# An encoder block on one Trainium2 core: where the last gate/up block turns its second pair, and where the last row of x joins its bank

## The chip, the cores and the metric

The kernel runs on one core of one Trainium2 chip. Its engines work side by side, each through its own list of instructions in order: TensorE (PE, matrix products into the eight PSUM banks), VectorE (DVE), ScalarE (ACT), GpSimd (POOL, which here mostly issues DMAs) and SyncE (SP, which issues the loads of weights). ACT and DVE also read PSUM. The metric is the time of one execution on the device in microseconds (us), a median over runs.

## The reference

One layer on x of 512 tokens by 2048, in float32:

```python
h = rmsnorm(x, g_mix)
qa, ka, va, qb, kb, vb = split(h @ w_in)
out_a = rmsnorm(mixer_a(qa, ka, va), g_out_a)   # grouped-query attention, axial rotary
out_b = rmsnorm(mixer_b(qb, kb, vb), g_out_b)   # three dilated windows, merged
x = x + concat(out_a, out_b) @ w_out
gate, up = split(rmsnorm(x, g_ffn) @ w_gate_up) # 2048 -> 2 x 5632
x = x + (silu(gate) * up) @ w_down              # 5632 -> 2048
return rmsnorm(x, g_final)
```

## The kernel before

**Products.** Each float32 factor is split into a high and a low part, and `mm3` makes a product from three matmuls of 128x128 by 128x512 (L228, L229, L230). The weights' high part is made by ACT (L837), the low part by DVE (L840), into tiles named `wide`. The large products go by a scheme of seven forms instead of eight blocks, named m1 to m7. A form is a sum of blocks of the activations times a sum of blocks of the weights (DVE makes the latter at L973). The forms share PSUM banks: m1, m6, m5 and m3 build on one another in the two banks of "z", m7 and m4 in those of "y", m2 in those of "x". So when m6 is complete its banks are read out, and m5 then accumulates onto the same banks.

**Units.** The program is a list of units; in the gate/up and down products a unit is one pair of rows of one form, six matmuls. The instructions of all engines are written out unit by unit. `box.after(form, late, f)` calls `f` `late` units behind the last unit of that form; the count runs on into the next block. This sets the order on every engine; there is no further scheduler.

**Gate/up and down.** Eleven gate/up blocks (`gate_up_block`) make four groups of 128 columns of silu(gate) * up each, as tiles `glo` and `uhi`. These must be turned (tokens from partitions to columns) to be the activations of the down product. The first ten blocks turn by DMA, the last one by PE: `turn_on_pe(k)` transposes one group with four matmuls (L1270) into a spare PSUM bank, and ACT copies it to a half of the tile `pair` (L1271). There is one such tile, `hpart[0]`. After two groups, `pair_sums` makes the sums that the forms need (four operations of DVE at L379), and `store` writes all seven forms of the pair to DRAM by a DMA from POOL (L1275). `next_forms` loads forms from there (`fr`, L1324) and splits them on ACT and DVE (L1327, L1330) into the `arena`.

The down product goes in blocks of 6, 8 and 8 pairs, twice each (two halves of the output's columns). The first block, of 6 pairs, has 42 units in this order: m1 and m7 mixed (12), m6 (6), two of m2, m5 (6), m2 and m4 mixed (6), m4 and m3 mixed (10). It begins right behind the last gate/up block, so "18 units behind m3" is the last unit of m6, and 34 units behind it the first unit of m3.

When a form of a down block is complete, ACT reads its two banks out (L1357), scaled, into an eviction tile from the ring `evs`, and POOL issues DMAs that add the tile to the output in DRAM (`x1d`, L1358). The ring begins with four tiles (`s6` and `ev`, two each). The four tiles of `s1` and `s7`, which hold `glo` and `uhi` until they are turned, join it later by the hook at L1473.

**The end.** The last down block does not write to DRAM; `put_row` (L1417) adds the banks to rows of x on the chip. Its m3 does the first row of tokens unit by unit and the second in `finish`, all at once, on a bank to which `seed_last` (L1443 to L1445, DVE) has added that row of x, divided by the row's scale. The row, `x1[3, 1]`, is the last of the rows that POOL loads from `x1d` (L1312). The order of this block is m1, m7, m6, two of m2, m5, m4, the rest of m2, m3, eight units a form.

Of the kernel before, what the change touches and what calls it, by code (L numbers as in the profile page):

```python
# [76 lines left out]
def encoder_block(ctx, tc, x, w_in, g_q_a, g_k_a, w_out, w_gate_up, w_down, g_final, x_t, gains, c_ident, c_mask,  # L77
# [36 lines left out]
    def small(n=4):  # L114
        used[0] += n
        assert used[0] <= 512
        return fixed[:, used[0] - n:used[0]]
# [118 lines left out]
    twins, evs, frs = [], [], []  # L236
# [919 lines left out]
    def pair_sums(w):  # L1156
        def part(n):
            return w[:, n * 256:(n + 1) * 256]
        a_r, a_l, s3, s2, b_l, b_r, s1, s4 = (part(n) for n in range(8))
        form_sums(a_l, a_r, b_l, b_r, s1, s2, s3, s4)  # L1160
# [41 lines left out]
    held = {}  # L1202

    def hold(name, shape, dtype=F32):
        if name not in held:
            held[name] = sp.tile([P] + list(shape), dtype, tag=name, bufs=1, name=nm(name))
        return held[name]

    forms_dram = dp.tile([P, 7, NFF // 2, 256], F32, tag="forms", name="forms")
    def gate_up_block(f0):  # L1210
        box = ColBlock(w_gate_up, 0, (f0 * P, DFF + f0 * P), KD // 2, REREAD, "craw40" if f0 == 40 else "craw", hf if f0 == 0 else None, two=True)
# [54 lines left out]
        def turn_on_pe(k):  # L1266
            ps, half = bank(), k % 2
            for n, t in enumerate((2, 3, 0, 1) if half == 0 else range(NT)):
                src = st[("glo", "uhi")[t // 2]][t % 2][:, k * P:(k + 1) * P]
                nc.tensor.transpose(ps[:, n * P:(n + 1) * P], src, ident)  # L1270
            nc.scalar.activation(hpart[0][:, half * 1024:half * 1024 + 512], ps, AF.Copy)  # L1271
            release(ps)

        def store(n):
            nc.gpsimd.dma_start(forms_dram[:, :, n], hpart[0][:, 256:].rearrange("p (f c) -> p f c", c=256))  # L1275
# [9 lines left out]
        box.after("m3", 1, low)  # L1285
        box.after("m3", 3, high)
        if f0 + 4 == NFF:
            for k, late in enumerate((6, 8, 18, 20)):
                box.after("m3", late, lambda k=k: turn_on_pe(k))
                if k % 2:  # L1290
                    box.after("m3", late + 2, lambda: pair_sums(hpart[0]))
                    box.after("m3", late + 5, lambda k=k: store((f0 + k) // 2))
            return box
# [10 lines left out]
    for f in range(0, NFF, 4):  # L1304
        box = gate_up_block(f)
# [3 lines left out]
    def load_x1(c, rows):  # L1309
        for t in rows:  # L1310
            x1.setdefault((c, t), slot("x1"))
            nc.gpsimd.dma_start(x1[c, t], x1_dram[c, t])  # L1312
# [31 lines left out]
    def down_block(first, pairs, cb, last):  # L1344
        box = ColBlock(w_down, 2 * first * P, (cb * 1024, cb * 1024 + 512), pairs, KEPT, f"draw{pairs}",
                       close=finish if last else None, two=True)

        def add(form, i, j):
            def go():
                for t in range(2):  # L1350
                    row = 2 * i + t
                    if not evs:
                        evs.extend(held["s6"][:, t] for t in range(2))
                        evs.extend(hold("ev", [2, 512])[:, t] for t in range(2))
                    evs.append(evs.pop(0))
                    e = evs[-1]
                    nc.scalar.activation(e, box.bank_of(form)[t], AF.Copy, scale=r2["r"][:, row:row + 1])  # L1357
                    nc.gpsimd.dma_start(x1_dram[2 * cb + j, row], e, accum_op=OP.add)  # L1358
                if form in LAST_OF_BANK:
                    box.done(form)  # L1360
            box.after(form, 0, go)

        def put(form, i, j):
            box.after(form, 0, lambda: [put_row(2 + j, 2 * i + t, box.bank_of(form)[t]) for t in range(2)])

        add("m1", 0, 0)
        add("m7", 1, 1)
        add("m6", 1, 0)
        if last:
            done_rows = [(c, t) for c in range(2) for t in (2, 3, 0, 1)]  # L1370
            for n in range(2):
                box.after("m7", 2 + 3 * n, lambda n=n: [load_gfin(n), load_x1(n, (2, 3)), load_x1(n, (0, 1))])
            box.after("m7", 7, lambda: [load_gfin(c) for c in (3, 2)])
            for n, (c, t) in enumerate(done_rows):
                box.after("m6", n - 2, lambda c=c, t=t: squares(c, t))
                box.after("m6", n, lambda c=c, t=t: gained(c, t))
            box.after("m6", 2, lambda: [load_x1(c, rows) for c, rows in ((3, (2, 3)), (2, (2, 3)), (2, (0, 1)), (3, (0, 1)))])
            put("m5", 1, 1)
            put("m4", 1, 0)
            box.after("m2", 0, last_weights)  # L1380
            put("m2", 0, 0)
            for t in range(2):
                box.after("m4", -4 + t, lambda t=t: gained(3, 2 + t))
                box.after("m2", 1 + t, lambda t=t: gained(2, t))
            box.after("m4", 1, lambda: [row_scale(t) for t in (2, 3)])
            box.after("m2", 3, lambda: seed_last(box.bank_of("m3")[1]))
            for n, (t, c) in enumerate(((2, 0), (2, 1), (3, 0), (3, 1))):
                box.after("m4", 2 + n, lambda t=t, c=c: [write(t, c, False, nc.sync), write(t, c + 2, True, nc.sync)])
        else:
            add("m2", 0, 0)  # L1390
            add("m5", 1, 1)
            add("m4", 1, 0)
            add("m3", 0, 1)
        return box
# [9 lines left out]
    def load_gfin(c):  # L1404
        gfin[c] = slot("gfin")
        nc.gpsimd.dma_start(gfin[c], row_bcast(g_final[c * 512:(c + 1) * 512], 512))
# [6 lines left out]
    def squares(c, t):  # L1413
        nc.scalar.activation(slot("jf"), x1[c, t], AF.Square, accum_out=sums_of(t)[:, c:c + 1])

    def put_row(c, t, ps):
        nc.vector.scalar_tensor_tensor(x1[c, t], ps, r2["r"][:, t:t + 1], x1[c, t], op0=OP.mult, op1=OP.add)  # L1417
        squares(c, t)

    def gained(c, t):  # L1420
        nc.vector.tensor_tensor(x1[c, t], x1[c, t], gfin[c], op=OP.mult)
        fin["y", c, t] = True

    def row_scale(t):
        tot = small(1)
        nc.vector.tensor_reduce(tot, fin[t], axis=AX.X, op=OP.add)
        fin["r", t] = rsqrt_mean(tot, 1, D)

    def write(t, c, vector, queue):
        r, y = fin["r", t], x1[c, t]  # L1430
        if ("y", c, t) not in fin:
            nc.vector.scalar_tensor_tensor(y, y, r, gfin[c], op0=OP.mult, op1=OP.mult)
        else:
            y = y if fin["y", c, t] is True else fin["y", c, t]
            if vector:
                nc.vector.tensor_scalar(y, y, r, None, op0=OP.mult)
            else:
                nc.scalar.activation(y, y, AF.Copy, scale=r)
        queue.dma_start(out[0, t * P:(t + 1) * P, c * 512:(c + 1) * 512], y)

    def seed_last(ps):
        r, q = r2["r"][:, 1:2], small(2)
        nc.vector.reciprocal(q[:, :1], r)  # L1443
        nc.vector.tensor_scalar(q[:, 1:], r, D ** -0.5, None, op0=OP.mult)
        nc.vector.scalar_tensor_tensor(ps, x1[3, 1], q[:, :1], ps, op0=OP.mult, op1=OP.add)  # L1445
        fin["mean"] = q[:, 1:]
# [23 lines left out]
        nc.vector.scalar_tensor_tensor(x1[3, 1], ps[1], m[:, 2:3], gfin[3], op0=OP.mult, op1=OP.mult)  # L1470
        nc.scalar.dma_start(out[0, P:2 * P, 3 * 512:], x1[3, 1])

    box.after("m3", 24, lambda: evs.extend(held[name][:, t] for name in ("s1", "s7") for t in range(2)))  # L1473
    first = 0
    for n in DOWN_PAIRS:
        next_forms(box, first, n)
        for cb in range(2):
            box = down_block(first, n, cb, (first + n, cb) == (NFF // 2, 1))
        first += n
# [149 lines left out]
```

## Time and profile before

| | before |
|---|---|
| median of 3 runs | 1963.26 us (1961.18 to 1963.49) |
| profiled execution | 1964.77 us, span 1963.0 us |
| instructions | 24580 |
| mean granted clock of TensorE | 0.996 |
| moved by DMA | 409.30 MB, 209 GB/s |

The span runs from the first to the last instruction of one profiled execution; the execution's time also has what lies around it. All times within the trace count from the span's start. An engine's busy time is the sum of its instructions; in a row of a timeline the bracket gives the time that the engine stood before the instruction, and what ended it. The granted clock is the share of TensorE's full clock that was let through.

### The profile page before, as it was taken

To read this page: it belongs to the slowest core of one execution; us is meant where nothing else is said; L and a number is where in the kernel's file an instruction comes from. 1 tells how busy PE (TensorE), PEld (TensorE's weight loads), DVE (VectorE), ACT (ScalarE), POOL (GpSimd) and SP (SyncE) were. 2 spreads that over 40 slices of the span, in tenths; PEclk is the share of its full clock that TensorE was granted. 3 is DMA by queue.
4 is the path that set the end of the run, shared out by engine and by line. 5 is a ranking of instruction groups with operands and counts; after the bars stand their busy time and mean duration, and the time that the engine had idled before them with its cause. 6 is when DMAs were issued, how large, how long until landed. Compare 5 with 4: busy or idle time off the path is not lost.

```text
span 1963.0 us, 24580 instructions
## 1 busy us (share of the span) xinstructions
PE 1941.8 (99%) x8743; PEld 1604.0 (82%) x8743; DVE 1536.9 (78%) x2012; ACT 1122.6 (57%) x1643; POOL 139.6 (7%) x184
## 2 busy tenths in 40 slices
PE   9999999999999999999999999999999899999998
PEld 7888888888888888888888888888888688888886
DVE  7987768787775697778778778778788778787886
ACT  7755554565455565555555555555555566555555
POOL 0000011000000000000000000000000121111121
PEclk9999999999999999999999999999999899999999
DMA  9677693144343566858758758767679688868865
GB/s 344 226 268 231 210 283 108 58 150 150 102 150 97 172 208 188 295 146 278 260 153 283 243 171 279 225 198 279 202 222 334 152 224 270 224 162 247 236 143 169
DMA packets 252028, 409.30 MB, mean 209 GB/s; under 512 B 58688, under 2 KB 85824, under 8 KB 251776
## 3 DMA queue, kind: packets, MB, share of 16 engines
q1 hardware_dynamic: 221072, 321.12, 50.1%
q0 software_dynamic: 22480, 60.57, 12.4%
q10 hardware_dynamic: 8352, 26.05, 4.1%
q8 instruction: 68, 1.11, 0.2%
q14 instruction: 56, 0.46, 0.1%
HBM read 334.52 MB, written 62.65 MB: 202 GB/s over the span
## 4 chain that ended last, share of the span: by engine, by line
PE 91%; issue 4%; DVE 3%; DMA 1%; ACT 1%; POOL 0%; DVEq 0%; POOLq 0%; SPq 0%; ACTq 0%
PE b L228 30%; PE b L229 30%; PE b L230 30%; PE b L613 1%; DMA forms<-pair 0%; PE b L1171 0%; PE b L563 0%; DVE x L1125 0%; PE b L790 0%; DVE w L306 0%; DVE ra L460 0%; DVE tw L896 0%; POOL x1d L1358 0%; DVE qA L463 0%; DMA stage<-in_w_in_dram 0%
## 5 line engine op out<-in xcount | busy, mean ns | idle before, releaser
L837 ACT ACTIVATE wide<-raw 128x1024 fp32r<-128x1024 f32 x462 | 487.0, 1059 | 456.5 <-PE b L230 271.1
L228 PE MATMUL b<-wide,arena 128*128 128x512 f32 x1848 | 721.7, 391 | 9.0 <-ACT s L1357 8.3
L840 DVE TENSOR_TENSOR wide<-raw,wide 128x1024 fp32r<-128x1024 f32 x462 | 562.1, 1221 | 213.9 <-ACT wide L837 207.5
L229 PE MATMUL b<-wide,arena 128*128 128x512 f32 x1848 | 720.8, 390 | 0.0
L230 PE MATMUL b<-wide,arena 128*128 128x512 f32 x1848 | 720.6, 390 | 0.0
L228 PEld LDWEIGHTS b<-wide,arena 128*128 128x128 f32 x1848 | 347.8, 188 | 81.4 <-ACT s L1357 8.6
L230 PEld LDWEIGHTS b<-wide,arena 128*128 128x128 f32 x1848 | 347.8, 188 | 72.3
L229 PEld LDWEIGHTS b<-wide,arena 128*128 128x128 f32 x1848 | 347.9, 188 | 71.6
L973 DVE TENSOR_TENSOR raw<-raw,raw 128x1024 f32<-128x1024 f32 x264 | 321.0, 1218 | 6.6 <-DMA raw<-in_w_gate_up_dram 6.6
L229 PE MATMUL b<-tw,arena 128*128 128x512 f32 x396 | 154.4, 390 | 0.6 <-DVE tw L896 0.6
L230 PE MATMUL b<-tw,arena 128*128 128x512 f32 x396 | 154.2, 389 | 0.0
L228 PE MATMUL b<-tw,arena 128*128 128x512 f32 x396 | 154.2, 389 | 0.0
L893 ACT ACTIVATE tw<-stage 128x512 fp32r<-128x512 f32 x140 | 85.4, 628 | 69.3 <-DVE stage L973 44.4
L896 DVE TENSOR_TENSOR tw<-stage,tw 128x512 fp32r<-128x512 f32 x140 | 93.5, 685 | 23.2 <-ACT tw L893 23.1
L228 PE MATMUL b<-w,arena 128*128 128x512 f32 x240 | 95.9, 400 | 0.0
L219 ACT ACTIVATE pTh<-b 128x512 fp32r<-128x512 f32 x64 | 38.2, 597 | 99.9 <-PE b L613 98.2
L230 PE MATMUL b<-w,arena 128*128 128x512 f32 x240 | 94.0, 392 | 0.0
L229 PE MATMUL b<-w,arena 128*128 128x512 f32 x240 | 93.6, 390 | 0.0
L229 PEld LDWEIGHTS b<-tw,arena 128*128 128x128 f32 x396 | 74.4, 188 | 16.8 <-DVE tw L896 1.4
L228 PEld LDWEIGHTS b<-tw,arena 128*128 128x128 f32 x396 | 74.4, 188 | 15.5
L230 PEld LDWEIGHTS b<-tw,arena 128*128 128x128 f32 x396 | 74.4, 188 | 15.2
L379 DVE TENSOR_TENSOR pair<-pair 128x256 f32<-128x256 f32 x120 | 46.4, 421 | 46.6 <-ACT pair L1174 23.2
(234 smaller groups left out, 2097.9 us busy)
## 6 DMA issues: line engine op xcount, KB each, us to landing
raw<-in_w_gate_up_dram SPq DMA_DIRECT2D x308, 512.0 KB, 6.2
raw<-in_w_down_dram SPq DMA_DIRECT2D x88, 512.0 KB, 7.7
stage<-in_w_in_dram SPq DMA_DIRECT2D x111, 256.0 KB, 5.4
forms<-pair POOLq DMA_DIRECT2D x22, 896.0 KB, 6.5
fr<-forms ACTq DMA_DIRECT2D x35, 512.0 KB, 5.0
raw<-in_w_out_dram SPq DMA_DIRECT2D x32, 512.0 KB, 4.2
x1d<-s POOLq DMA_DIRECT2D x56, 256.0 KB, 6.8
stage<-in_w_in_dram SPq DMA_DIRECT2D x90, 128.0 KB, 3.5
```

The lines of the kernel that those rows point to most:

```text
L219: nc.scalar.activation(hi, src, AF.Copy)
L228: nc.tensor.matmul(dst, ah, bh, start=start, stop=False, skip_group_check=chained)
L229: nc.tensor.matmul(dst, ah, bl, start=False, stop=False, skip_group_check=chained)
L230: nc.tensor.matmul(dst, al, bh, start=False, stop=stop, skip_group_check=chained)
L379: nc.vector.tensor_tensor(out, x, y, op=op)
L613: nc.tensor.transpose(ps[:, t * P:(t + 1) * P], self.p[t][:, kb * P:(kb + 1) * P], ident)
L837: nc.scalar.activation(self.hi, self.src, AF.Copy)
L840: nc.vector.tensor_tensor(self.lo, self.src, f32(self.hi), op=OP.subtract)
L893: nc.scalar.activation(self.pair[:, 0], self.src, AF.Copy)
L896: nc.vector.tensor_tensor(self.pair[:, 1], self.src, f32(self.pair[:, 0]), op=OP.subtract)
L973: nc.vector.tensor_tensor(t[dst], t[src[0]], t[src[1]], op=OP.add if form == "m6" else OP.subtract)
```

## The change

Three hooks are given other places. In the last gate/up block (`f0 + 4 == NFF`) the third and fourth group are turned 34 and 36 units behind its m3 instead of 18 and 20; the sums follow two units and the store five units behind the fourth group, so they move along. The tiles of `s1` and `s7` join the eviction ring 40 units behind it instead of 24. In the last down block, `seed_last` is called five units behind m5 instead of three behind m2.

```diff
         if f0 + 4 == NFF:
-            for k, late in enumerate((6, 8, 18, 20)):
+            for k, late in enumerate((6, 8, 34, 36)):
                 box.after("m3", late, lambda k=k: turn_on_pe(k))
                 if k % 2:
                     box.after("m3", late + 2, lambda: pair_sums(hpart[0]))
                     box.after("m3", late + 5, lambda k=k: store((f0 + k) // 2))
...
-            box.after("m2", 3, lambda: seed_last(box.bank_of("m3")[1]))
+            box.after("m5", 5, lambda: seed_last(box.bank_of("m3")[1]))
...
-    box.after("m3", 24, lambda: evs.extend(held[name][:, t] for name in ("s1", "s7") for t in range(2)))
+    box.after("m3", 40, lambda: evs.extend(held[name][:, t] for name in ("s1", "s7") for t in range(2)))
```

The order on ACT around the end of m6 in the first down block; `b_78` and `b_71` are the banks of the turned groups, `b_72` and `b_76` those of m6, `s_546` an eviction tile:

```order
 L1327 ACTIVATE arena_85<-fr_10982 128x4x256
 L837 ACTIVATE wide_5846<-raw_5908 128x1024
-L1271 ACTIVATE pair_5381<-b_78 128x512
 L1357 ACTIVATE s_546_6203<-b_72,fixed 128x512
 L1357 ACTIVATE s_546_6203<-b_76,fixed 128x512
 L837 ACTIVATE wide_5840<-raw_5739 128x1024
 L1324 DMA fr_10982<-forms 128x1024
-L1271 ACTIVATE pair_5381<-b_71 128x512
 L1327 ACTIVATE arena_85<-fr_10983 128x2x256
```

The copy of the third group stood ahead of the evictions of m6 and stands there no more; that of the fourth has gone from behind them.

ACT sixteen units later, behind the evictions of m2, and ahead of those of m4:

```order
 L837 ACTIVATE wide_5846<-raw_5906 128x1024
+L1271 ACTIVATE pair_5381<-b_75 128x512
 L837 ACTIVATE wide_5840<-raw_5940 128x1024
+L1271 ACTIVATE pair_5381<-b_71 128x512
 L837 ACTIVATE wide_5842<-raw_5908 128x1024
```

Both copies now stand here, each between two splits of weights, out of banks `b_75` and `b_71`.

POOL's DMAs in the same part; `s_546` and `ev` are eviction tiles, and the rows with `x1d` add them to the output in DRAM, for m2, m4 and m3 in turn:

```order
 L1358 DMA x1d_122<-s_546_6203 128x512
 L1358 DMA x1d_123<-s_546_6203 128x512
+L1358 DMA x1d_124<-ev_11330 128x512
+L1358 DMA x1d_125<-ev_11330 128x512
+L1275 DMA forms<-pair_5381 896x1x256
+L1358 DMA x1d_126<-s_546_6203 128x512
+L1358 DMA x1d_127<-s_546_6203 128x512
```

The second pair's store, which stood behind m6's DMAs, now stands between those of m4 and m3, and these two take their tiles from the ring of four (before, they had `s1` and `s7`).

DVE in the last down block; `b_77` is the bank that the seed goes to, `x_638` the last row of x:

```order
 L840 TENSOR_TENSOR wide_5847<-raw_13693,wide_5846 128x1024
 L1421 TENSOR_TENSOR x_632_13748<-x_632_13748,gfin_13703 128x512
+L1443 RECIPROCAL fixed<-fixed 128x1
+L1444 TENSOR_SCALAR fixed<-fixed 128x1
+L1445 SCALAR_TENSOR_TENSOR b_77<-x_638_13760,fixed,b_77 128x512
 L840 TENSOR_TENSOR wide_5841<-raw_13723,wide_5840 128x1024
```

The three operations of the seed stood ahead of the last `put_row`, behind all splits of weights; they now have six splits behind them.

## The prediction

> **What bounds the kernel now.** The page comes first, then the waits of TensorE (PE):
>
> ```profile
> PE 1941.8 (99%) x8743; PEld 1604.0 (82%) x8743; DVE 1536.9 (78%) x2012; ACT 1122.6 (57%) x1643; POOL 139.6 (7%) x184
> PE 91%; issue 4%; DVE 3%; DMA 1%; ACT 1%; POOL 0%; DVEq 0%; POOLq 0%; SPq 0%; ACTq 0%
> PE b L228 <- ACT s L1357: 8.3, 1, 8.3
> PE b L228 <- DVE b L1445: 0.6, 1, 0.6
> ```
>
> PE is busy for 99% of the span and makes 91% of the chain that ended last, so a microsecond in which PE does not wait is a microsecond of the span, and hardly anything else is. PE waits long only once, 8.3 us, for the eviction at L1357; the other wait that the change touches is 0.6 us for the seed at L1445. The timelines of the engines show how the long one comes about (start, length, engine, line, idle time before it and what ended it):
>
> ```profile
> 1536.07 1.54 DVE L379 TENSOR_TENSOR pair<-pair 128x256 f32<-128x256 f32 x4
> 1542.43 1.74 POOL L1358 DMA_DIRECT2D x1d<-ev  x2 [4.31 <-ACT ev L1357]
> 1550.31 0.94 POOL L1275 DMA_DIRECT2D forms<-pair  x1 [6.14 <-DVE raw L973]
> 1546.40 1.06 ACT L837 ACTIVATE wide<-raw 128x1024 fp32r<-128x1024 f32 x1 [0.26 <-DVE raw L973]
> 1557.88 0.60 ACT L1271 ACTIVATE pair<-b 128x512 f32<-128x512 f32 x1 [10.42 <-DMA forms<-pair]
> 1558.37 1.26 ACT L1357 ACTIVATE s<-b,fixed 128x512 f32<-128x512 f32 x2
> 1550.19 0.60 PE L1270 MATMUL b<-fixed,s 128*128 128x128 f32 x4
> 1559.11 0.79 PE L228 MATMUL b<-wide,arena 128*128 128x512 f32 x1 [8.32 <-ACT s L1357]
> ```
>
> The first pair's sums (L379) were done at 1537.6, but its store was issued only at 1550.31, 6.1 us after POOL's accumulating DMAs, and landed at about 1557.8. ACT's copy of the second pair (L1271) writes the same single tile `pair`, so it stood from 1547.5 to 1557.88 for that landing. Queued right behind it were the evictions of m6's banks (L1357), which PE needs before m5 may accumulate there. PE stood until 1559.11 and then ran slowly. Busy time and instructions by engine (PE, PEld, DVE, ACT, POOL), then granted clock, DMA share and GB/s:
>
> ```profile
> 1555.00:1559.10 4.10, 0.00 (x0) 0.00 (x0) 0.00 (x0) 1.22 (x3) 0.00 (x0) 0.51 0.45 164
> 1559.10:1565.30 6.20, 6.19 (x15) 4.84 (x16) 4.66 (x8) 3.59 (x6) 1.77 (x2) 0.50 0.87 165
> 1565.30:1570.00 4.70, 4.70 (x22) 3.91 (x21) 4.65 (x5) 3.10 (x4) 0.94 (x1) 1.00 0.76 227
> ```
>
> After the stand PE had half its clock for 6.2 us more: 15 matmuls there, 22 in the shorter stretch behind it.
>
> **The change part by part.** *The second pair's turn, 16 units later.* The waiting copy no longer stands ahead of m6's evictions on ACT (first piece of the order above). What they now wait for is PE's end of m6, at about 1547.1, so both are done by about 1548.7, while PE has two units of m2 (12 matmuls, 2.7 us) before m5. The gain is read from the starts of PE's matmuls:
>
> ```profile
> 1546.98 0.60 PE L1270 MATMUL b<-fixed,s 128*128 128x128 f32 x4
> 1547.33 0.48 PE L228 MATMUL b<-wide,arena 128*128 128x512 f32 x1
> 1549.96 0.39 PE L230 MATMUL b<-wide,arena 128*128 128x512 f32 x1
> 1565.51 0.40 PE L228 MATMUL b<-wide,arena 128*128 128x512 f32 x1
> ```
>
> Behind four transposes the next matmul starts after 0.35 us (1546.98 to 1547.33). Behind those at 1550.19 it took 8.92 us, so the stand costs 8.92 - 0.35 = 8.57 us. From 1559.11 to 1565.51 are 15 starts, 6.40 us. At full clock, 11 starts took 2.63 us (1547.33 to 1549.96), and four more at 0.23 us make 3.55 for 15. The slow clock therefore costs 6.40 - 3.55 = 2.85 us. With PE never idle here, nothing in the trace would lower the clock: the share is 1.00 in every stretch of this stage in which PE does not stand.
>
> The Trainium skill's page "TensorE: Matmul & The Clock Gate" (Part 1: The HAM clock gate) says that the clock halves after an idle window of about 3.4 us and is whole again after about 3.4 us of work. The halving agrees (0.51 and 0.50 after the stand); the length does not, 6.2 us here. By the page's length the clock term would be an estimated 1.7 us instead of 2.85, and the time 1.15 us later than I forecast.
>
> The transposes, the two copies and the sums are moved, not added. The copies now come behind m2's evictions, the store behind m4's DMAs and ahead of m3's (second and third piece). PE's transposes take two banks that nothing has used since the first pair's turn, so PE does not wait for them. ACT's loads of `fr`, which stood behind the waiting copy, leave earlier, and none stands behind it at the new place; SP's order is the same. The copy still waits for the first store. Sixteen units of six matmuls at 0.23 us are 22 us, so it comes at about 1569, and the landing at 1557.8 has 11 us to spare. For what lies beside it:
>
> ```profile
> 1545.00:1550.00 5.00, 5.00 (x26) 4.12 (x25) 5.00 (x6) 2.20 (x3) 0.00 (x0) 1.00 0.98 193
> 1570.00:1575.00 5.00, 5.00 (x23) 4.15 (x23) 2.09 (x2) 3.02 (x5) 1.73 (x2) 1.00 0.99 261
> 1580.00:1585.00 5.00, 5.00 (x23) 4.13 (x22) 3.46 (x3) 3.88 (x5) 1.73 (x2) 1.00 0.95 288
> 1585.00:1590.00 5.00, 5.00 (x24) 4.13 (x22) 2.63 (x4) 2.71 (x5) 1.39 (x2) 1.00 1.07 318
> 1600.00:1605.00 5.00, 5.00 (x24) 4.15 (x23) 4.63 (x4) 2.41 (x4) 0.11 (x1) 1.00 0.05 11
> ACT wide L837 <- DMA raw<-in_w_down_dram: 0.3, 1, 0.3
> 1565.89 0.94 POOL L1275 DMA_DIRECT2D forms<-pair  x1 [4.67 <-issue]
> 1571.72 0.87 POOL L1358 DMA_DIRECT2D x1d<-ev  x1 [4.88 <-ACT ev L1357]
> ```
>
> The four sums (1.54 us) leave a stretch where VectorE (DVE) had no free time (5.00 of 5) and enter one with 3.9 us free in ten (1580 to 1590): price zero. If that cover were gone, at most 1.54; nothing to win either, since PE did not wait where they were. The copies (two of 0.6) find ACT 3.4 us free there. In the gap DVE stood too, waiting for ACT; what it loses is the 2.85 us of slow matmuls in which it could get ahead. Between 1570 and 1575 it was idle 2.9 us for want of work, so I take zero and keep 2.85 as the upper end.
>
> The store moves past three pairs of accumulating DMAs on POOL. A store and the DMA behind it were 5.8 us apart (1565.89 to 1571.72), so m3's pair may leave some 10 us later than before: the store first waits for m4's pair to land, as the first one did. Their tiles are wanted again a whole block later. Its own 0.9 MB meets full DMA engines (1.07), but ACT waited for weights only 0.3 us in this stage, and at 1600 to 1605 they stand empty. Zero again, with 1 us as the upper end, as no PE wait came from weights.
>
> *The eviction ring.* Until unit 40 it has four tiles, so m3's eviction reuses the tile of m2's:
>
> ```profile
> 1579.76 1.25 ACT L1357 ACTIVATE s<-b,fixed 128x512 f32<-128x512 f32 x2
> 1580.72 1.73 POOL L1358 DMA_DIRECT2D x1d<-s  x2 [7.27 <-ACT s L1357]
> 1591.56 1.37 ACT L1357 ACTIVATE s<-b,fixed 128x512 f32<-128x512 f32 x2 [0.81 <-PE b L230]
> DMA to landing us min/median/max: 4.0/6.5/10.0
> ```
>
> The last row is for the accumulating DMAs between 1530 and 1610. By the median, m2's pair lands at about 1588; by the longest at 1591.4, just ahead of 1591.56. I take zero. The upper end is a wait of a few us on ACT, of which PE sees only what exceeds ACT's lead; in the old wait PE stood 8.32 of ACT's 10.42, so the lead was 2.1.
>
> *The seed.* It moves on DVE from m3's third unit to m4's fifth (last piece). The tail in starts of PE's matmuls, and what lies beside the new place:
>
> ```profile
> 1947.90 0.39 PE L229 MATMUL b<-wide,arena 128*128 128x512 f32 x1
> 1948.13 0.39 PE L230 MATMUL b<-wide,arena 128*128 128x512 f32 x1
> 1949.16 0.50 PE L228 MATMUL b<-wide,arena 128*128 128x512 f32 x1 [0.64 <-DVE b L1445]
> 1949.97 0.39 PE L228 MATMUL b<-wide,arena 128*128 128x512 f32 x1
> 1925.00 1.70 POOL L1312 DMA_DIRECT2D x<-x1d  x3 [0.42 <-issue]
> x<-x1d POOLq DMA_DIRECT2D x16, 256.0 KB, 4.6
> 1934.28 1.43 DVE L1417 SCALAR_TENSOR_TENSOR x<-b,fixed,x 128x512 f32<-128x512 f32 x2 [2.39 <-PE b L230]
> ```
>
> From 1948.13 to 1949.97 are four starts in 1.84 us; at 0.23 each they take 0.92, so 0.92 us goes, and the final chain hangs on PE's last matmul. The last row of x comes with the last of the loads at 1926.2, so with 4.6 us at about 1930.8, when DVE reaches the seed (about 1930.6). A late row holds the weights' split behind it, covered by the 2.39 us that DVE stood before 1934.28. Lower end zero, upper 0.92; I take 0.92.
>
> **The sum.** 8.57 + 2.85 + 0.92 = 12.3 us. The profiled execution took 1964.77 (span 1963.0, 1.8 around it): 1952.4 after. It lies 1.5 over the median of the runs, 1963.26, to which I refer the forecast: 1951.0.
>
> **The rivals.** (a) *The cover is gone*: with PE running on, DVE and ACT come late between 1550 and 1600. For it speaks DVE's 5.00 of 5; against it, that PE waited for no split there, and that DVE had idle time 20 us later. Price 2.85 to 4.4 (plus the sums' 1.54), so 1954 to 1955.5; with a second loss of clock 1957. A store that delays weights ends in the same place. The page "DMA: Bandwidth & Descriptors" (Queues, rings and completion order) says that each DMA engine takes turns between queues packet by packet, so by it the store does slow the loads beside it; no row here gives that price.
>
> (b) *The change does not remove the wait*: something else holds m6's evictions as long. The copy was the only instruction ahead of them that waited for a DMA, and nothing replaces it. Only the seed's gain would stay: 1962.3.
>
> (c) *Slower*: the ring of four tiles. If m2's pair lands late, ACT stands at m3's eviction with the weights' copies behind it. To lose more than was won, PE would have to stand over 9.5 us (2.85 of clock on top), ACT over 11.6, so the landing would be at 1603, some 21 us after the issue; the longest took 10.0. If so, 1964 to 1967.
>
> **Chances.** The forecast 0.77, its own range 1949.5 to 1953.1: 1.2 us to each side for the runs' spread (1961.18 to 1963.49), 0.92 up if the seed brings nothing, 0.25 down if the clock costs half of its whole 6.2 us. (a) 0.14, (b) 0.05, (c) 0.04. The range for 8 in 10 reaches into (a): 1949.0 to 1955.5 (half a us below the forecast's own). This kernel's measurement can tell about 0.2%, 3.9 us, from no change. The forecast and (a) lie beyond that, 0.91 faster; (b) is the same, with a little of (c), 0.06; the rest of (c) 0.03 slower.
>
> **What the profile after should show.** No PE wait for L1357; granted clock 1.00 from 1530 to 1600; m5's first matmul right behind m2's second unit; ACT's L1271 of the second pair ended by PE's transposes instead of the store; the second store issued once m4's DMAs have landed; no PE wait for L1445. The prediction is wrong if PE waits for L840, L837 or an eviction between 1550 and 1610, or if DVE stands for `x<-x1d` at the seed for over 2.4 us.

## The result, and the profile after

The changed kernel takes 1952.09 us (median of 4 runs, 1951.01 to 1953.56) against 1962.3 of the kernel before in the same comparison (1961.18 to 1963.49): ratio 0.9948, 95% interval 0.9931 to 0.9966. It is 10.2 us faster, 0.34 to 0.69%. The forecast was 1951.0 with a range of 1949.0 to 1955.5. The profiled execution took 1951.23 us, its span 1949.4.

The page after (engines, then the chain):

```profile
PE 1937.3 (99%) x8743; PEld 1599.7 (82%) x8743; DVE 1536.5 (79%) x2012; ACT 1123.3 (58%) x1643; POOL 140.1 (7%) x184
PE 96%; DVE 3%; issue 1%; ACT 0%; DMA 0%; DVEq 0%; POOLq 0%; POOL 0%; SPq 0%; ACTq 0%
```

The longest waits of PE over the whole run (waited for: us in total, times, longest):

```profile
PE b L186 <- DVE warm L181: 1.3, 1, 1.3
PE b L229 <- DVE tw L896: 0.6, 2, 0.3
```

PE has gone from 91 to 96% of the chain, and the waits for L1357 (8.3 us) and L1445 (0.6) are gone. From 1500 to 1960 no wait of PE is left at all. The timelines of ACT, POOL and DVE at the places that were changed:

```profile
1546.10 1.25 ACT L1357 ACTIVATE s<-b,fixed 128x512 f32<-128x512 f32 x2
1568.26 0.59 ACT L1271 ACTIVATE pair<-b 128x512 f32<-128x512 f32 x1
1571.43 0.60 ACT L1271 ACTIVATE pair<-b 128x512 f32<-128x512 f32 x1 [0.70 <-PE b L1270]
1578.95 1.37 ACT L1357 ACTIVATE s<-b,fixed 128x512 f32<-128x512 f32 x2 [0.81 <-PE b L230]
1548.72 0.94 POOL L1275 DMA_DIRECT2D forms<-pair  x1 [5.82 <-DVE raw L973]
1557.58 1.77 POOL L1358 DMA_DIRECT2D x1d<-s  x2 [7.92 <-ACT ev L1357]
1584.90 0.94 POOL L1275 DMA_DIRECT2D forms<-pair  x1 [6.97 <-DVE wide L840]
1589.91 1.76 POOL L1358 DMA_DIRECT2D x1d<-s  x2 [4.06 <-ACT wide L837]
1917.73 0.76 DVE L1445 SCALAR_TENSOR_TENSOR b<-x,fixed,b 128x512 f32<-128x512 f32 x1
```

m6's evictions start at 1546.10, not 1558.37, and no longer stand behind a copy. The copies (L1271) wait for PE's transposes at most, no longer for the store. The second store leaves 6.97 us behind POOL's issue for m4, m3's DMAs at 1589.91, 9.6 us after ACT was done with that tile (1580.3), and nobody waits for them: m3's eviction itself waited only for PE. The seed runs at 1917.73 without a wait. By stretches (columns as before: length; PE, PEld, DVE, ACT, POOL; granted clock, DMA share, GB/s):

```profile
1545.00:1550.00 5.00, 5.00 (x24) 4.14 (x23) 5.00 (x6) 3.74 (x6) 0.94 (x1) 1.00 0.88 210
1555.00:1560.00 5.00, 5.00 (x24) 4.14 (x23) 4.69 (x4) 4.17 (x6) 2.42 (x3) 1.00 0.84 271
```

PE is busy throughout at a granted clock of 1.00, with DVE close to full.

**Where the profiled pair's 13.5 us come from.** Three instructions that both traces have, first of before, then of after (the first split of weights behind the transposes, the last split that waits, the last operation of DVE):

```profile
1531.09 1.06 ACT L837 ACTIVATE wide<-raw 128x1024 fp32r<-128x1024 f32 x1 [3.03 <-PE b L1270]
1944.21 1.23 DVE L840 TENSOR_TENSOR wide<-raw,wide 128x1024 fp32r<-128x1024 f32 x1 [0.81 <-ACT wide L837]
1957.43 0.74 DVE L1470 SCALAR_TENSOR_TENSOR x<-b,fixed,gfin 128x512 f32<-128x512 f32 x1
```

```profile
1529.82 1.06 ACT L837 ACTIVATE wide<-raw 128x1024 fp32r<-128x1024 f32 x1 [3.03 <-PE b L1270]
1931.60 1.23 DVE L840 TENSOR_TENSOR wide<-raw,wide 128x1024 fp32r<-128x1024 f32 x1 [0.81 <-ACT wide L837]
1943.88 0.74 DVE L1470 SCALAR_TENSOR_TENSOR x<-b,fixed,gfin 128x512 f32<-128x512 f32 x1
```

The distances are 1.27, 12.61 and 13.55 us. So 1.27 us lie ahead of the change and have nothing to do with it; 11.34 belong to the turn (8.57 + 2.85 = 11.42 in the forecast) and 0.94 to the seed (0.92).

### The profile page after: what moved, and what is told of

The parts are those of the page before. It is cut to its first block, busy times and chain, and to the rows that moved or that the text cites. A ratio compares the mean times of both kernels' runs of the same rounds, so it can differ in the third digit from the quotient of the medians.

```text
span 1949.4 us, 24583 instructions
## 1 busy us (share of the span) xinstructions
PE 1937.3 (99%) x8743; PEld 1599.7 (82%) x8743; DVE 1536.5 (79%) x2012; ACT 1123.3 (58%) x1643; POOL 140.1 (7%) x184
## 4 chain that ended last, share of the span: by engine, by line
PE 96%; DVE 3%; issue 1%; ACT 0%; DMA 0%; DVEq 0%; POOLq 0%; POOL 0%; SPq 0%; ACTq 0%
PE b L228 31%; PE b L230 31%; PE b L229 31%; PE b L613 1%; PE b L1171 0%; PE b L563 0%; DVE x L1125 0%; DVE w L306 0%; DVE ra L460 0%; DVE tw L896 0%; DVE qA L463 0%; PE b L790 0%; DMA stage<-in_w_in_dram 0%; PE b L574 0%; DVE qA L469 0%
```

## The experiments

The 1.27 us made a measure necessary that leaves the start of the program out: from POOL's first accumulating DMA of the first down block to the end of the span. In after that is 1949.4 - 1534.99 = 414.4 us. All medians and ratios are over 5 to 11 runs beside 11 to 21 runs of the kernel before (medians 1962.0 to 1962.7).

| kernel | median us | against before | ratio, 95% interval | first x1d DMA to end |
|---|---|---|---|---|
| before | | | | 426.7 |
| after | 1952.09 | -10.2 | 0.9948 (0.9931 to 0.9966) | 414.4 |
| e1: turn alone | 1953.46 | -9.0 | 0.9953 (0.9939 to 0.9967) | 415.2 |
| e2: seed alone | 1961.28 | -1.2 | 0.9996 (0.9987 to 1.0005) | 425.4 |
| e3: turn at 26, 28 | 1952.59 | -9.8 | 0.9954 (0.9941 to 0.9966) | 415.4 |
| e4: turn at 22, 24 | 1960.87 | -1.6 | 0.9987 (0.9979 to 0.9996) | 423.4 |
| e5: the same, ring at 26 | 1954.96 | -7.7 | 0.9960 (0.9947 to 0.9972) | 417.1 |
| e6: second tile | 1953.51 | -9.1 | 0.9952 (0.9940 to 0.9965) | 415.3 |
| e7: first store early | 1954.18 | -8.5 | 0.9954 (0.9940 to 0.9967) | 415.9 |
| e8: first store twice | 1967.68 | +5.0 | 1.0027 (1.0017 to 1.0038) | 431.0 |
| e9: first store in two | 1957.43 | -4.6 | 0.9971 (0.9961 to 0.9981) | 419.5 |
| e10: ring alone | 1962.08 | +0.1 | 0.9998 (0.9989 to 1.0007) | 424.6 |

**The change in parts (e1, e2, e10).** Each of the three hooks alone, in the kernel before.

```diff
-            for k, late in enumerate((6, 8, 18, 20)):
+            for k, late in enumerate((6, 8, 34, 36)):
-    box.after("m3", 24, lambda: evs.extend(
+    box.after("m3", 40, lambda: evs.extend(
```

> The kernel before with the turn of the second pair alone at 34 and 36 units (and the ring's hook at 40); the seed stays three units behind m2. My theory: the stand of 8.57 us and the 2.85 us of slow clock go, nothing else: 11.4 us less than before, 1950.9 against 1962.3, ratio 0.9942; the trace has no PE wait for L1357 and keeps the 0.6 us wait for L1445. Rival (b'), the gain came from the seed or from elsewhere in the run (start-up): under 4 us less. Rival (a), the cover is partly gone and the seed hid it: 7 to 9 us less, with PE waits for L840 or L837 between 1545 and 1610.

9.0 us less, with an interval of about 6.5 to 12; in the traces 426.7 - 415.2 = 11.5. No PE wait for L1357, and the wait for the seed (0.6 us) is kept. The turn carries nearly all of the gain. The 2 us between median and trace are taken up below.

```diff
-            box.after("m2", 3, lambda: seed_last(box.bank_of("m3")[1]))
+            box.after("m5", 5, lambda: seed_last(box.bank_of("m3")[1]))
```

> The kernel before with only the seed moved to five units behind m5. My theory: 0.92 us less, which the comparison can hardly tell from none (1961.4 against 1962.3, ratio 0.9995); the trace shows it: no PE wait for L1445, and the four starts of PE ahead of the tail 0.23 us apart instead of 1.84 us for four. Rival: the seed waits for the last row of x and holds the splits of weights behind it, so PE waits for L840 there: 0 to 2 us more.

The time cannot tell 0.92 us from none, as expected; in its trace PE waits for nothing from 1900 on. The rival had one thing half right. DVE does wait for a row of x, but it is an earlier one, and for 1.22 us that reach no wait of PE (before, it waited 0.49 us there, so the seed is not the whole of it):

```profile
1922.57 1.41 DVE L1417 SCALAR_TENSOR_TENSOR x<-b,fixed,x 128x512 f32<-128x512 f32 x2 [1.22 <-DMA x<-x1d]
```

```diff
-    box.after("m3", 24, lambda: evs.extend(
+    box.after("m3", 40, lambda: evs.extend(
```

> The kernel before with only the ring's hook moved from 24 to 40 units, so that m3's eviction takes m2's tiles. My theory: m2's pair leaves about 1580.7 and lands about 1588, ahead of m3's eviction at 1591.6: no wait, no change, 1962.4, and the trace shows the stand of the first store once more (8 us, with half clock behind it). Rival: the pair lands late, as in the kernel with the turn at 22 units; then ACT stands there for a DMA x1d<-s, and it is 1 to 6 us more.

No change, as my theory had it. This run gives one more execution of the old stand, and a shorter one:

```profile
1557.05 0.60 ACT L1271 ACTIVATE pair<-b 128x512 f32<-128x512 f32 x1 [8.62 <-DMA forms<-pair]
```

```profile
PE b L228 <- ACT s L1357: 6.6, 1, 6.6
```

**What makes the copy wait (e6, e7, e9, e8).** First, a tile of its own for the second pair, with the turn left where it was. Two forms' unused rows of the arena serve for it; the copies and sums are rounded there, and the store is two DMAs:

```diff
-            nc.scalar.activation(hpart[0][:, half * 1024:half * 1024 + 512], ps, AF.Copy)
+            nc.scalar.activation(hpart[0][:, half * 1024:half * 1024 + 512] if k < 2 else spare(half * 1024, 512), ps, AF.Copy)
...
+                        box.after("m3", late + 2, spare_sums)
+                        box.after("m3", late + 5, spare_store)
```

> The kernel before, but the second pair gets a tile of its own (two forms' unused rows of the arena, which the last gate/up block has read and the first down block does not use); its two copies and sums are rounded to the short form there, which changes the result a little, and its store is two DMAs. The turn stays at 18 and 20 units. My theory, that ACT's copy waits only because both pairs share one tile: no wait of the copy, none of PE, the whole 11.4 us less (1951.0, ratio 0.994), though the turn is not moved. Rival, that the turn at this place costs by itself (ACT's time, or the banks): at least a part of the 11.4 us stays, 1954 to 1962.

ACT's timeline in this kernel (L1276 is the copy, L1377 the eviction):

```profile
1547.26 0.60 ACT L1276 ACTIVATE arena<-b 128x512 fp32r<-128x512 f32 x1
1547.76 1.26 ACT L1377 ACTIVATE s<-b,fixed 128x512 f32<-128x512 f32 x2
```

The copy at its old place waits for nothing, and the kernel is as fast as with the turn moved: 415.3 against 415.2. So the place costs nothing by itself; the shared tile did.

Then the first store three units earlier, between m1's and m7's DMAs on POOL:

```diff
-                    box.after("m3", late + 5, lambda k=k: store((f0 + k) // 2))
+                    box.after("m3", late + (2 if k == 1 else 5), lambda k=k: store((f0 + k) // 2))
```

> The kernel before with the first pair's store three units earlier (right behind its sums, so that it stands between m1's and m7's accumulating DMAs on POOL instead of behind m7's); nothing else. My theory, that the store was late because of the DMAs ahead of it on POOL's queue: it leaves when m1's DMAs have landed, about 1541 to 1542 instead of 1550.3, and lands at about 1549; the copy stands 1.5 us at most, under ACT's lead of 2.1, PE not at all: 11.4 us less, 1951 to 1952. m7's DMAs then leave behind it, at about 1549. Rival A, that the store starts as soon as its sums are done (1537.7) and nothing on the queue holds it: it lands about 1545, the same time. Rival B, that the store leaves late for another reason than its place in the queue: no change, 1962.3. Rival C, that m7's late DMAs hold m5's eviction, which takes their tiles: a PE wait for L1357 near 1560 of 1 to 4 us, 1952 to 1958.

```profile
1537.24 1.86 POOL L1358 DMA_DIRECT2D x1d<-s  x2 [50.38 <-ACT s L1357]
1544.22 0.95 POOL L1275 DMA_DIRECT2D forms<-pair  x1 [5.12 <-issue]
1551.11 1.74 POOL L1358 DMA_DIRECT2D x1d<-ev  x2 [5.94 <-issue]
1550.89 0.60 ACT L1271 ACTIVATE pair<-b 128x512 f32<-128x512 f32 x1 [3.10 <-DMA forms<-pair]
1552.12 0.50 PE L228 MATMUL b<-wide,arena 128*128 128x512 f32 x1 [0.16 <-ACT s L1357]
```

The store leaves at 1544.22 instead of 1550.31, which rules out rival B; it does not leave when its sums are done, which rules out rival A. It leaves 2 to 3 us later than I said, 5.12 us behind the issue of m1's pair, and ACT stands 3.10 us. PE sees 0.16 of it, so ACT's lead is 2.9 us here (2.1 in the prediction). Rival C did not occur. Nearly the whole gain, with the turn unmoved.

Whether the store waited because of its size or because of its place in the queue, a division into two DMAs tells:

```diff
+            for lo, hi in parts:
+                nc.gpsimd.dma_start(forms_dram[:, lo:hi, n], src[:, lo:hi])
...
+                    box.after("m3", late + 5, lambda k=k: store((f0 + k) // 2, ((0, 3), (3, 7)) if k == 1 else ((0, 7),)))
```

> The kernel before with the first pair's store issued as two DMAs, three forms and then four, one behind the other at the old place. In the runs so far a store of seven forms never left POOL while accumulating DMAs issued ahead of it were still under way, while a third accumulating DMA, or a store of three forms, did leave right behind two of them. My theory, that POOL's queue holds only so many rows under way at a time and the whole store is too large to share it: the piece of three leaves right behind m7's pair, about 1544, the piece of four when that pair has landed, about 1550; with less left to move it lands some 3 us earlier than the whole store, ACT's copy stands 7 us instead of 10.4, PE 5 instead of 8.3: 3 to 5 us less than before, 1957.5 to 1959.5. Rival, that a store waits for the landing of what is ahead of it whatever its size: the first piece leaves at 1550, the second at some 1555, and the landing is as late or later: 0 to 3 us more.

```profile
1542.39 1.73 POOL L1360 DMA_DIRECT2D x1d<-ev  x2 [4.32 <-ACT ev L1359]
1543.61 1.32 POOL L1277 DMA_DIRECT2D forms<-pair  x1
1550.79 0.84 POOL L1277 DMA_DIRECT2D forms<-pair  x1 [5.86 <-issue]
1551.49 0.60 ACT L1271 ACTIVATE pair<-b 128x512 f32<-128x512 f32 x1 [4.08 <-DMA forms<-pair]
1557.90 0.60 ACT L1271 ACTIVATE pair<-b 128x512 f32<-128x512 f32 x1 [3.71 <-DMA forms<-pair]
```

Three forms leave right behind m7's pair, the other four 5.86 us after that issue ended: size decides, not order alone. The time, 1957.43, is just below the expected 1957.5 to 1959.5, but by a path that I had not worked out: the first copy needs only the first piece to have landed, so ACT's stand is split in two, 4.08 and 3.71 us. PE's waits from 1500 to 1700:

```profile
PE b L228 <- ACT s L1359: 1.8, 1, 1.8
PE b L229 <- DVE wide L840: 1.6, 1, 1.6
```

Neither lowers the clock, so 4.3 us (419.5 - 415.2) are all that is left of the 11.5.

Last, the suspected cost doubled:

```diff
                     box.after("m3", late + 5, lambda k=k: store((f0 + k) // 2))
+                    if k == 1:
+                        box.after("m3", late + 5, lambda k=k: store((f0 + k) // 2))
```

> The kernel before with the first pair's store issued twice, one behind the other: the suspected wait is made longer by one store. My theory: the second leaves some 0.3 us after the first has landed and takes 7.5 us, so ACT's copy and PE's stand last 7.5 us more, and the slow clock behind it costs the same 2.85 us as before: 7.5 us more than before, 1970, with half clock for some 6.2 us again. Rival, that the clock's loss grows with the stand: 2.5 us on top, 1972.4. Rival, that the two stores run beside each other: 0 to 2 us more.

```profile
1549.20 0.94 POOL L1275 DMA_DIRECT2D forms<-pair  x1 [6.38 <-DVE raw L973]
1556.75 0.94 POOL L1275 DMA_DIRECT2D forms<-pair  x1 [6.62 <-DMA forms<-pair]
1561.56 0.60 ACT L1271 ACTIVATE pair<-b 128x512 f32<-128x512 f32 x1 [15.44 <-DMA forms<-pair]
```

```profile
PE b L228 <- ACT s L1359: 13.4, 1, 13.4
```

Slower, and by the stand alone: PE stands 5.0 us longer, and the time is 5.0 us longer by the medians, 4.3 by the traces. My 7.5 was too much: the second store took 4.8 us until the copy could start (1556.75 to 1561.56), the first 7.5 until the second could (1549.20 to 1556.75). Neither rival holds: the stores did not run beside each other, and the slow clock behind the stand cost less than before, not more (below). Both stores write the same rows of DRAM, so that the second waits for the first says nothing of the queue.

**How much later the turn must come (e3, e4, e5).** The edit is e1's with other numbers: (6, 8, 26, 28), and (6, 8, 22, 24).

> The kernel before with the second pair turned at 26 and 28 units instead of 18 and 20 (ring's hook at 40, seed left). Eight units of 1.38 us later, ACT reaches the copy about 1558, counted as in the profile of before, where the first store lands at 1557.8. My theory, that only the landing of the first store counts: no PE wait, the whole 11.4 us less (1950.9, ratio 0.9942), as with 34 units. Rival, that ACT or DVE is too short of time between 1550 and 1565 for the copies and the sums there: PE waits for L837 or L840 of 1 to 3 us, 1952 to 1954. Rival, that the store lands later when PE does not stand, since the weights then come faster: ACT stands 2 to 5 us and PE 0 to 3.

Eight units are enough: 415.4 us against 415.2. The first copy waits last for PE:

```profile
1557.42 0.60 ACT L1271 ACTIVATE pair<-b 128x512 f32<-128x512 f32 x1 [1.65 <-PE b L1270]
```

The margin is small. The store landed at 1556.7 (1548.77 and 7.9 us from issue to landing), 0.9 us after ACT was ready for the copy, and only PE's transposes, which came later still, hid that. At 34 units the landing has 10.9 us to spare (1557.3 in after, where the copy starts at 1568.26). The first rival falls. The second has its premise right: the store took 7.9 to 9.3 us to land where PE did not stand meanwhile (after, e1, e3, e4, e5, e6) and 6.0 to 7.5 where it did (before, e2, e8, e10). The reason was not tried, and here PE lost nothing by it.

> The kernel before with the second pair turned at 22 and 24 units. ACT reaches the copy about 1552.5 to 1553 and stands 4.7 us for the store. My theory: PE sees this less a lead of ACT of about 2.1 us, so a stand of about 2.6 us for a split of weights (not for L1357), and as it is short, no slow clock: 11.4 - 2.6 = 8.8 us less than before, 1953.5. Rival, that any stand of some us brings the half clock: 2.85 us more, 1956.4, with a stretch of granted clock 0.5 of some 6 us. Rival, that ACT's lead is over 4.7 us at this place: no stand, 1950.9.

```profile
1559.26 0.60 ACT L1271 ACTIVATE pair<-b 128x512 f32<-128x512 f32 x1 [6.90 <-PE b L230]
1590.07 0.69 ACT L1357 ACTIVATE s<-b,fixed 128x512 f32<-128x512 f32 x1 [8.15 <-DMA x1d<-s]
1564.05 1.72 POOL L1358 DMA_DIRECT2D x1d<-ev  x2 [2.81 <-ACT ev L1357]
1576.22 0.94 POOL L1275 DMA_DIRECT2D forms<-pair  x1 [10.45 <-DVE wide L840]
1585.84 1.77 POOL L1358 DMA_DIRECT2D x1d<-s  x2 [8.68 <-issue]
1594.14 0.49 PE L228 MATMUL b<-wide,arena 128*128 128x512 f32 x1 [2.61 <-ACT wide L837]
```

I was wrong by 7 us. The first loss came out near the expected one because two errors cancelled. ACT stood 6.90 us instead of 4.7 (the row puts it down to PE, whose transposes had long been done at 1553.3), since the store took 9.3 us to land; and PE lost some 2.3 us by the starts of its matmuls, at full clock, so ACT's lead at this place was 4.6 us, not 2.1. A second came 30 us later, and it is rival (c) of the prediction: ACT stood for `x1d<-s` before m3's eviction. The second store now stands ahead of m2's DMAs on POOL. m2 is read out by 1573.7, but its DMAs leave only at 1585.84, and with four tiles m3 must wait for them. (The new kernel's m2 pair leaves at 1567.20, 1.0 us behind the eviction's start.) PE waits 2.6 and 0.8 us, and its clock then halves for 3.4 us. With the ring's hook at 26:

> As the kernel with the turn at 22 and 24 units, but the ring's hook at 26 instead of 40, so m3 evicts into other tiles than m2's. My theory: of that kernel's two losses the second (ACT 8.15 and 1.70 us at m3's eviction for the landing of m2's pair, PE 2.6 and 0.8 us) goes, with its stretch of clock 0.66, and the first (some 2.5 us of PE around 1561 to 1567) stays: 11.4 - 2.5 = 8.9 us less than before, some 1953.5. Rival, that the second store delays more than the ring (weights or forms): a loss of some us between 1585 and 1605 stays, 1956 to 1961.

The second loss is gone, the first stays at 1.9 us (417.1 - 415.2). Its price is thus 423.4 - 417.1 = 6.3 us in the traces, 5.9 in the medians. It need not be the same each time: four of e4's eleven runs took 1957.4 to 1958.4 us, the others 1960.2 to 1962.8, and the traced run (1961.50) is one of these.

## Why the prediction was right, step by step

**The stand.** Cause and size hold. Removing the turn's place (e1), the tile's sharing (e6) or the store's lateness (e7) each brings it down to 0.2 us or nothing.

**The slow clock.** The term exists but is no constant. I read its 2.85 us as what follows a stand. The clock changes in steps; stretches at half clock, cut at its changes (one run each: before, e2, e10, e8, e4):

```profile
1555.06:1565.30 10.24, 6.19 (x15) 4.84 (x16) 4.66 (x8) 4.81 (x8) 1.77 (x2) 0.50 0.70 162
```

```profile
1553.56:1563.80 10.24, 5.27 (x12) 4.12 (x13) 3.73 (x7) 4.65 (x7) 1.77 (x2) 0.50 0.76 193
```

```profile
1556.74:1563.57 6.83, 5.29 (x13) 4.13 (x14) 3.75 (x7) 4.65 (x7) 1.77 (x2) 0.50 0.80 148
```

```profile
1553.77:1567.42 13.65, 4.63 (x11) 3.67 (x12) 3.09 (x6) 4.65 (x7) 2.80 (x3) 0.50 0.65 174
```

```profile
1596.53:1599.94 3.41, 3.41 (x10) 2.64 (x9) 3.29 (x3) 2.11 (x2) 0.00 (x0) 0.50 0.93 187
```

They last 3, 3, 2, 4 and 1 times 3.41 us. What PE works at half clock is what is left of the step in which it resumes, and one whole step: 6.19, 5.27, 5.29 and 4.63 us after the stands, or a loss of half that time. The Trainium skill's page "TensorE: Matmul & The Clock Gate" (Part 1: The HAM clock gate) says that the window is 3413 ns and free-running. The five stretches agree with the length; and the clock halved 3.2 us (e2) to 5.0 us (e10) after PE had stopped, at no fixed distance. The prediction set its 3.4 us against my 6.2 and found that they differ, which was my misreading: 6.2 is a remainder and a whole window. That the prediction's other estimate, with 1.7 us for the clock, would have come out at the measured 1952.1 is chance: the clock cost half of 4.6 to 6.2 us, 2.3 to 3.1.

**The sum against the median.** Here a size was off. I took 11.4 us from one execution (1964.77 us, above all four runs of its series) off the median. Three executions of the old stage are to be had: 426.7 in before, 425.4 + 0.92 (the seed) = 426.3 in e2, 424.6 in e10; against the mean of the three without a stand (e1, e3, e6: 415.3) they lose 11.4, 11.0 and 9.3. The landing of the store and the phase of the clock vary. So 10.6 on average, and the medians say 9.0 to 9.8 for the turn alone, with intervals that include 10.6. The forecast came out 1.1 us low, inside its own range. Part of that closeness is luck: it took 12.3 us off a median of 1963.26, while the gain was 10.2 us off 1962.3, the median of before with a fourth run. The forecast gain was thus 2.1 us too large, and a base 1.0 us too high hid half of it.

**What I took as zero.** Right: sums, copies, weights behind the store, the cover of DVE and ACT; no wait of PE is left from 1500 to 1960. Rivals (a) and (b) fall.

**The eviction ring.** Zero was right, but the point from which it decides was not. I let m2's DMAs leave right behind their eviction and asked how long they would take. In e4 they left 12 us behind it because the store stood ahead of them, and that was enough. The changed kernel has the store behind m4's DMAs, where it delays only m3's own. The ring of four has little to spare even so: ACT stood 0.58 us for m6's DMAs at m2's eviction in e1, and 0.61 us for m4's at the next block's first eviction in e3. PE lost nothing by either.

**The seed.** 0.94 us for 0.92 in the traces; no series of runs here can show it by time.

No version in these runs beats the changed kernel beyond their intervals; e3 and e6, which reach the same stage without a stand, keep the old seed.

## What to carry to other kernels

When an engine waits for a DMA only because two users share one tile, look for the cheapest of three cures: a later second user, an earlier DMA, or another tile; here each of them won 8.5 to 9.8 us. Moving a large DMA in a queue can bring a second, distant wait through a ring of few tiles: look at what is queued behind the new place, not only at what was queued behind the old one. Take the size of a stall from several executions where they are to be had, for its length and the slow clock behind it vary by 2 us here.

## What the runs showed of the hardware that I had not expected

POOL's queue takes only a limited amount at a time. A whole store (seven forms, 0.9 MB) behind accumulating DMAs never left within 3.7 us of POOL's last issue (3.78 in e9, 5.12 in e7, 6.14 in before, 10.45 in e4), while three forms left 1.2 us after the first of two accumulating DMAs had (e9). Of accumulating DMAs three went together and a fourth did not:

```profile
1559.19 1.77 POOL L1358 DMA_DIRECT2D x1d<-s  x2 [7.87 <-ACT ev L1357]
1560.28 1.55 POOL L1358 DMA_DIRECT2D x1d<-ev  x1
1567.58 0.84 POOL L1358 DMA_DIRECT2D x1d<-ev  x1 [5.75 <-ACT wide L837]
```

These are e1's. What the limit counts (rows, bytes or DMAs) was not tried.

A stand need not be one piece to lower the clock: in e4 PE was busy for 1.62 us of the 3.41 before the half clock, in two waits with a few matmuls between them; e9's two waits of 1.8 and 1.6 us, 10 us apart, left it at 1.00.
